# Moving the product of the gate's second half from sixth to fourth place in a seven-product feed-forward pair

## The chip, the cores and the metric

The kernel runs on one core of one Trainium2 chip. The metric is device time in microseconds for one execution, median of several. A profile of one execution gives, for each engine, when every instruction started and how long it took. The engines are called PE (TensorE's matmuls), PEld (its weight loads), DVE (VectorE), ACT (ScalarE), POOL (GpSimd) and SP (the queue that issues most DMAs).

## What is computed

The reference runs two transformer blocks of two layers each on one sequence of 512 tokens of width 1024. Layers differ in their mixers (mLSTM and neighbourhood attention, differential attention, HGRN2, forgetting attention, RG-LRU, stick-breaking attention), but each of the four layers ends in the same feed-forward part, and only that part is touched here:

```python
def swiglu(x, w_gu, w_down):
    gate, up = jnp.split(x @ w_gu, 2, axis=-1)
    return (jax.nn.silu(gate) * up) @ w_down
```

The hidden width is 2816, that is 22 blocks of 128. All of it is float32.

## The kernel before

Values lie transposed: 128 channels on the partitions, 512 tokens along the free side. A float32 factor is split into a high part (a copy by ACT into a reduced float32 type) and a low part (a subtraction by DVE), in the helper `split` at lines 271 to 278 (its copy is L273, its subtraction L275). A product of two split factors is three matmuls, high by high, high by low, low by high, issued by `mm3` (L283, L284, L285).

`ffn` (from L651) works through the 22 hidden blocks in three parts of 8, 7 and 7. A part first makes its hidden blocks, then multiplies them by its share of the down weights (L700 and on). The first three blocks of the first part are made in the plain way. The other 19 blocks of each layer, 76 in the kernel, are made by `seven` (L584 to L649), one call for each pair of a gate block and an up block. It is a scheme of Strassen's kind: gate and up for one hidden block are a 2 by 2 arrangement of half-size products (half the 1024 channels, half the 512 tokens), and seven such products replace eight. Each product is 12 matmuls of 128 x 128 weights by 256 columns (four channel blocks, three matmuls each).

In a call of `seven`, `g` and `u` are the gate and up weights as loaded by SP's queue (L607, L608). `a1` is the split of `g`. `ss` (from `s12`) and `a2` (from what is left in `u`) are splits of sums and differences of the halves of `g` and `u`, made by DVE on L612 to L617; `a4` is the split of the second half of `g` after L617. `b11`, `b12`, `b21`, `b22` are the four quarters of x, `t1` to `t4` are sums of them, made once in a feed-forward part (their high parts lie in the tile `ao`, their low parts in `t_l`). The products are, in the order in which the code writes them:

- P1: `a1` first half by `b11`, into the accumulator `pa` (a PSUM bank, tile `p_sc` in the profile). ACT copies `pa` to `keep[0]` (L630).
- P2: `ss` second half by `t2`, added onto `pa`. ACT copies `pa` to `keep[1]` (L633).
- P3: `ss` first half by `t1`, into `pz` (tile `p_tp`).
- P4: `a2` first half by `t3`, added onto `pa`. ACT copies `pa` to `keep[2]` (L636), and DVE adds `keep[2]` and `pz` into `c22` (L637).
- P5: `a1` second half by `b21`, into `pb` (tile `p_mm`). DVE adds `keep[0]` and `pb` (L639), ACT applies Silu (L640).
- P6: `a2` second half by `t4`, added onto `pa`. DVE multiplies it in (L642).
- P7: `a4` by `b22`, added onto `pz`, then L646 to L648 finish the second 256 tokens and `sink` splits the hidden block (tiles `f_h`, `f_l`).

`pa` thus holds a running sum that is read off three times in the middle of its accumulation: a product that adds onto `pa` can start only when the copy of the sum before it has ended. `seven` is a generator: `ffn` runs P1 of a pair, then P7 of the pair before, then P2 to P6, so TensorE sees P1, P7 of the pair before, P2, P3, P4, P5, P6, and then P1 of the next pair. The sets of weights are double-buffered: `a1` has two buffers, `ss` and `a2` share a ring of four.

What order an engine really issues in is decided by the layer under the kernel, which plans the whole program before it runs. For each engine it takes the instructions in the order of the program, but where the next one would have to wait by the planner's own estimate of durations, it puts a later one that is ready in its place, single matmuls too. That order is then fixed; on the chip each engine follows it and waits on semaphores.

Of the kernel before, what the change touches and what calls it, by code (L numbers as in the profile page):

```python
# [11 lines left out]
AF = mybir.ActivationFunctionType  # L12
ALU = mybir.AluOpType
# [193 lines left out]
class Prog:  # L207
# [376 lines left out]
    def seven(self, gate, up, pool, ts, sink):  # L584


        nc = self.nc
        t1, t2, t3, t4 = ts
        x = [[(self.XH[k][:, c], self.XL[k][:, c]) for k in range(4 * i, 4 * i + 4)] for i in range(2) for c in (slice(0, 256), slice(256, S))]
        b11, b12, b21, b22 = x  # L590
        h1, h2 = slice(0, 512), slice(512, 1024)

        def parts(src, own=None, bufs=4):

            tags, home, n = (("w_hi", "w_lo"), self.wp, 1024) if own is None else ((own + "h", own + "l"), pool, src.shape[1])
            hi, lo = (home.tile([P, n], F32R, name=i, tag=i, bufs=bufs) for i in tags)
            self.split(hi, lo, src)
            return hi, lo

        def product(ps, w, c, b, first, last):  # L600
            for k in range(4):
                ws = slice(c.start + k * P, c.start + (k + 1) * P)
                self.mm3(ps, (w[0][:, ws], w[1][:, ws]), b[k], first and k == 0, last and k == 3, skip_group_check=not (first and last))

        g = self.wp.tile([P, 1024], F32, name="w_raw", tag="w_raw", bufs=3)
        u = pool.tile([P, 1024], F32, name="u_raw", tag="u_raw", bufs=2)
        nc.sync.dma_start(out=g, in_=gate)  # L607
        nc.sync.dma_start(out=u, in_=up)  # L608
        a1 = parts(g, "a1", 2)
        s12 = pool.tile([P, 1024], F32, name="s12", tag="s12", bufs=1)  # L610

        nc.vector.tensor_tensor(s12[:, h1], u[:, h1], u[:, h2], ALU.add)  # L612
        nc.vector.tensor_tensor(s12[:, h2], s12[:, h1], g[:, h1], ALU.subtract)
        ss = parts(s12)
        nc.vector.tensor_tensor(u[:, h1], g[:, h1], u[:, h1], ALU.subtract)
        a2 = parts(u)
        nc.vector.tensor_tensor(g[:, h2], g[:, h2], s12[:, h2], ALU.subtract)  # L617

        pa = self.mm("sc")[:, 0:256]
        pz = self.mm("tp")[:, 0:256]  # L620
        pb = self.mm("mm")[:, 0:256]
        keep = []
        for name, bufs in (("k1", 1), ("k2", 2), ("k3", 1)):
            keep.append(pool.tile([P, 256], F32, name=name, tag=name, bufs=bufs))
        s = self.fp.tile([P, S], F32, name="f_s", tag="f_s", bufs=2)
        c22 = pool.tile([P, 256], F32, name="c22", tag="c22", bufs=1)
        c0, c1 = slice(0, 256), slice(256, S)

        product(pa, a1, h1, b11, True, False)
        nc.scalar.activation(keep[0], pa, AF.Copy)  # L630
        yield
        product(pa, ss, h2, t2, False, False)
        nc.scalar.activation(keep[1], pa, AF.Copy)  # L633
        product(pz, ss, h1, t1, True, False)
        product(pa, a2, h1, t3, False, False)
        nc.scalar.activation(keep[2], pa, AF.Copy)  # L636
        nc.vector.tensor_tensor(c22, keep[2], pz, ALU.add)  # L637
        product(pb, a1, h2, b21, True, True)
        nc.vector.tensor_tensor(s[:, c0], keep[0], pb, ALU.add)  # L639
        nc.scalar.activation(s[:, c0], s[:, c0], AF.Silu)  # L640
        product(pa, a2, h2, t4, False, True)
        nc.vector.tensor_tensor(s[:, c0], s[:, c0], pa, ALU.mult)  # L642
        a4 = parts(g[:, h2], "s4", 1)
        yield
        product(pz, a4, h1, b22, False, True)
        nc.vector.tensor_tensor(s[:, c1], keep[1], pz, ALU.add)  # L646
        nc.scalar.activation(s[:, c1], s[:, c1], AF.Silu)
        nc.vector.tensor_tensor(s[:, c1], s[:, c1], c22, ALU.mult)  # L648
        sink(s)  # L649
# [1072 lines left out]
```

## Time and profile before

| | us |
|---|---|
| Median of three runs | 2801.26 (2798.82 to 2802.35) |
| The profiled execution: its own time | 2803.35 |
| Its span, first to last instruction | 2801.6 |
| PE busy | 2751.7 (98%) |
| DVE busy | 2039.3 (73%) |
| ACT busy | 1513.2 (54%) |
| POOL busy | 415.8 (15%) |

The profiled execution's own time is 2.1 us above the median of the runs. Matmuls overlap in the records: one of 256 columns is recorded as 276 to 283 ns, while the next one starts 113 to 118 ns after it. The distance between starts, not the recorded length, is what a matmul costs.

### The profile page before, as it was taken

Reading aid. Unit: us, or ns where it says so; the run is one execution under the profiler, and the core shown is the slowest. Engines: PE = TensorE matmul, PEld = TensorE weight load, DVE = VectorE, ACT = ScalarE, POOL = GpSimd, SP = SyncE. Lnnn points to the kernel's source line nnn. Section 1 sums busy time; section 2 is a strip of 40 time slices with the busy share of each in tenths; the row PEclk is TensorE's granted clock in tenths of the full one; section 3 lists DMA queues with packets and bytes.
Section 4 is the critical chain, followed back from the end, with each engine's and each line's share of the span. In section 5 each row is a group of like instructions: output and inputs, shape, how many; then the busy total and the mean of one; then the engine's idle time right before and its main releaser. Section 6 shows DMA issues by size and latency. Waiting matters only on the chain. (4 is left out here: it accounts for less than half of the span.)

```text
span 2801.6 us, 46515 instructions
## 1 busy us (share of the span) xinstructions
PE 2751.7 (98%) x18090; PEld 2460.9 (88%) x18090; DVE 2039.3 (73%) x3560; ACT 1513.2 (54%) x2800; POOL 415.8 (15%) x500
## 2 busy tenths in 40 slices
PE   9999999999999999999999999999999999999998
PEld 7778989999987678899999988799999977898998
DVE  5877657776767888568667767778677758696785
ACT  4556545453556776455445544655445548663553
POOL 0412103000021122030000333240000301300003
PEclk9999999999999999999999999999999999999999
DMA  5232412323332225214232321224232321132322
GB/s 180 79 116 92 153 65 84 122 90 100 98 109 87 85 66 166 77 61 136 90 114 80 108 77 61 83 69 136 83 114 87 102 91 46 59 114 92 113 86 74
DMA packets 83103, 269.50 MB, mean 96 GB/s; under 512 B 10649, under 2 KB 15145, under 8 KB 82881
## 3 DMA queue, kind: packets, MB, share of 16 engines
q1 hardware_dynamic: 81376, 261.49, 28.8%
q0 software_dynamic: 1504, 5.04, 0.6%
q8 instruction: 142, 2.33, 0.3%
q14 instruction: 81, 0.66, 0.1%
HBM read 260.14 MB, written 2.15 MB: 94 GB/s over the span
## 5 line engine op out<-in xcount | busy, mean ns | idle before, releaser
L349 DVE TENSOR_TENSOR w_lo<-w_raw,w_hi 128x1024 fp32r<-128x1024 f32 (+3 forms) x440 | 412.2, 959 | 220.6 <-ACT w_hi L347 212.7
L347 ACT ACTIVATE w_hi<-w_raw 128x1024 fp32r<-128x1024 f32 (+2 forms) x326 | 331.6, 1024 | 364.5 <-PE p_mm L284 168.3
L283 PE MATMUL p_mm<-xh,w_hi 128*128 128x256 f32 (+1 forms) x1312 | 450.4, 344 | 9.6 <-ACT w_hi L347 5.1
L284 PE MATMUL p_mm<-xl,w_hi 128*128 128x256 f32 (+1 forms) x1312 | 447.5, 341 | 0.7 <-DVE xl L275 0.6
L285 PE MATMUL p_mm<-xh,w_lo 128*128 128x256 f32 (+1 forms) x1312 | 446.3, 340 | 0.0
L283 PEld LDWEIGHTS p_mm<-xh,w_hi 128*128 128x128 f32 x1312 | 248.9, 190 | 36.8 <-ACT w_hi L347 5.1
L284 PEld LDWEIGHTS p_mm<-xl,w_hi 128*128 128x128 f32 x1312 | 249.2, 190 | 29.0 <-DVE xl L275 1.7
L285 PEld LDWEIGHTS p_mm<-xh,w_lo 128*128 128x128 f32 x1312 | 249.2, 190 | 27.3 <-DVE w_lo L349 1.1
L510 POOL TENSOR_TENSOR ao<-xf 128x256 f32<-128x256 f32 x20 | 17.4, 871 | 1656.8 <-DVE xf L503 1227.8
L283 PE MATMUL p_sc<-ao,w_hi 128*128 128x256 f32 x912 | 256.5, 281 | 0.7 <-ACT k L630 0.7
L284 PE MATMUL p_sc<-t_l,w_hi 128*128 128x256 f32 x912 | 254.8, 279 | 0.0
L285 PE MATMUL p_sc<-ao,w_lo 128*128 128x256 f32 x912 | 254.8, 279 | 0.0
L283 PEld LDWEIGHTS p_sc<-ao,w_hi 128*128 128x128 f32 x912 | 173.1, 190 | 2.6 <-ACT k L630 2.5
L284 PEld LDWEIGHTS p_sc<-t_l,w_hi 128*128 128x128 f32 x912 | 171.4, 188 | 0.0
L285 PEld LDWEIGHTS p_sc<-ao,w_lo 128*128 128x128 f32 x912 | 171.2, 188 | 0.0
L284 PE MATMUL p_mm<-f_l,w_hi 128*128 128x512 f32 (+1 forms) x464 | 156.5, 337 | 1.4 <-DVE f_l L275 1.4
L283 PE MATMUL p_mm<-f_h,w_hi 128*128 128x512 f32 (+1 forms) x464 | 157.0, 338 | 0.0
L285 PE MATMUL p_sc<-f_h,w_lo 128*128 128x512 f32 (+1 forms) x464 | 156.4, 337 | 0.1
L283 PE MATMUL p_sc<-f_h,w_hi 128*128 128x512 f32 (+1 forms) x464 | 156.1, 337 | 0.0
L285 PE MATMUL p_mm<-f_h,w_lo 128*128 128x512 f32 (+1 forms) x464 | 156.1, 336 | 0.0
L284 PE MATMUL p_sc<-f_l,w_hi 128*128 128x512 f32 (+1 forms) x464 | 155.9, 336 | 0.0
L505 ACT ACTIVATE ao<-xf 128x256 f32<-128x256 f32 x160 | 64.8, 413 | 118.8 <-DVE xf L499 61.2
(497 smaller groups left out, 8011.5 us busy)
## 6 DMA issues: line engine op xcount, KB each, us to landing
w_raw<-in_f_gu SPq DMA_DIRECT2D x100, 512.0 KB, 3.6
u_raw<-in_f_gu SPq DMA_DIRECT2D x76, 512.0 KB, 3.5
w_raw<-in_w_e SPq DMA_DIRECT2D x70, 512.0 KB, 3.5
w_raw<-in_w_x SPq DMA_DIRECT2D x64, 512.0 KB, 3.9
w_raw<-in_w_o SPq DMA_DIRECT2D x64, 512.0 KB, 3.6
w_raw<-in_f_d SPq DMA_DIRECT2D x64, 448.0 KB, 3.3
w_raw<-in_f_d SPq DMA_DIRECT2D x32, 512.0 KB, 3.5
r_s<-r_t SPq DMA_DIRECT2D x64, 64.0 KB, 2.0
```

What stands on the lines that cost most here:

```text
L283: nc.tensor.matmul(out, wh, xh, start=start, stop=False, **kw)
L284: nc.tensor.matmul(out, wh, xl, start=False, stop=False, **kw)
L285: self.last = nc.tensor.matmul(out, wl, xh, start=False, stop=stop, **kw)
L347: nc.scalar.activation(hi[:, :n], raw[:, :n], AF.Copy)
L349: nc.vector.tensor_tensor(lo[:, c], raw[:, c], hi[:, c].bitcast(F32), ALU.subtract)
L505: square = nc.scalar.activation(x2, self.XF[m][:, c], AF.Square)
L510: eng.tensor_tensor(sm, self.XF[order[0]][:, c], self.XF[m][:, c], ALU.add)
```

## The change

P5, with the DVE addition and the Silu that follow from it, is moved from behind P4's read-out to in front of P3. No instruction is added or removed. The order that the code writes becomes P1, P7 of the pair before, P2, P5, P3, P4, P6: with P7 of the pair before counted in, the moved product comes fourth instead of sixth.

```diff
         yield
         product(pa, ss, h2, t2, False, False)
         nc.scalar.activation(keep[1], pa, AF.Copy)
+        product(pb, a1, h2, b21, True, True)
+        nc.vector.tensor_tensor(s[:, c0], keep[0], pb, ALU.add)
+        nc.scalar.activation(s[:, c0], s[:, c0], AF.Silu)
         product(pz, ss, h1, t1, True, False)
         product(pa, a2, h1, t3, False, False)
         nc.scalar.activation(keep[2], pa, AF.Copy)
         nc.vector.tensor_tensor(c22, keep[2], pz, ALU.add)
-        product(pb, a1, h2, b21, True, True)
-        nc.vector.tensor_tensor(s[:, c0], keep[0], pb, ALU.add)
-        nc.scalar.activation(s[:, c0], s[:, c0], AF.Silu)
         product(pa, a2, h2, t4, False, True)
```

## Rows read from the trace of the kernel before

**Rows 1.** The page's first part: busy time, share, instructions of each engine

```profile
PE 2751.7 (98%) x18090; PEld 2460.9 (88%) x18090; DVE 2039.3 (73%) x3560; ACT 1513.2 (54%) x2800; POOL 415.8 (15%) x500
```

**Rows 2.** Windows, six pairs in a row: length, each engine's busy time, granted clock

```profile
589.54:648.06 58.52, 58.52 (x506) 58.52 (x505) 49.39 (x80) 34.95 (x59) 0.00 (x0) 1.00 0.36 116
```

**Rows 3.** Timeline, PE, one pair's products (start, length, engine, line, tiles)

```profile
599.29 0.28 PE L283 MATMUL p_sc<-xh,a1h 128*128 128x256 f32 x1
...
600.66 0.28 PE L283 MATMUL p_tp<-xh,s4h 128*128 128x256 f32 x1
...
602.02 0.28 PE L283 MATMUL p_sc<-ao,w_hi 128*128 128x256 f32 x1
...
604.85 0.28 PE L283 MATMUL p_sc<-ao,w_hi 128*128 128x256 f32 x1
...
606.26 0.28 PE L283 MATMUL p_mm<-xh,a1h 128*128 128x256 f32 x1
...
607.68 0.28 PE L283 MATMUL p_sc<-ao,w_hi 128*128 128x256 f32 x1
...
609.05 0.28 PE L283 MATMUL p_sc<-xh,a1h 128*128 128x256 f32 x1
```

**Rows 4.** Timeline, PE, the first product of two neighbouring pairs, second layer

```profile
1293.21 0.28 PE L283 MATMUL p_sc<-xh,a1h 128*128 128x256 f32 x1
...
1302.91 0.28 PE L283 MATMUL p_sc<-xh,a1h 128*128 128x256 f32 x1
```

**Rows 5.** Timeline, ACT, beside the pair of Rows 3 (idle before, its releaser, in brackets)

```profile
604.42 0.63 ACT L273 ACTIVATE f_h<-f_s 128x512 fp32r<-128x512 f32 x1 [0.24 <-DVE f_s L648]
605.08 1.06 ACT L273 ACTIVATE w_hi<-s 128x1024 fp32r<-128x1024 f32 x1
606.52 0.38 ACT L636 ACTIVATE k<-p_sc 128x256 f32<-128x256 f32 x1 [0.38 <-PE p_sc L285]
607.76 1.06 ACT L273 ACTIVATE a1h<-w_raw 128x1024 fp32r<-128x1024 f32 x1 [0.85 <-PE p_mm L284]
608.73 0.40 ACT L640 ACTIVATE f_s<-f_s 128x256 f32<-128x256 f32 x1
```

**Rows 6.** Source line L636, the copy after P4: count, ns min/median/max

```profile
L636 ACT ACTIVATE k<-p_sc x76: 359/384/387, 494.3 to 2742.6; 128x256 f32<-128x256 f32 x76
```

**Rows 7.** Timeline, DVE, the low part of the next pair's `a1`

```profile
599.10 1.23 DVE L275 TENSOR_TENSOR a1l<-w_raw,a1h 128x1024 fp32r<-128x1024 f32 x1 [0.56 <-ACT a1h L273]
```

**Rows 8.** Timeline, first pair of a part: end of P1, copy, start of P2

```profile
582.13 0.28 PE L285 MATMUL p_sc<-xh,a1l 128*128 128x256 f32 x1
...
582.25 0.28 PE L283 MATMUL p_tp<-ao,w_hi 128*128 128x256 f32 x1
...
582.45 0.38 ACT L630 ACTIVATE k<-p_sc 128x256 f32<-128x256 f32 x1 [0.53 <-PE p_sc L285]
...
582.60 0.28 PE L283 MATMUL p_tp<-ao,w_hi 128*128 128x256 f32 x1
...
582.88 0.38 PE L283 MATMUL p_sc<-ao,w_hi 128*128 128x256 f32 x1
...
583.10 0.28 PE L284 MATMUL p_sc<-t_l,w_hi 128*128 128x256 f32 x1
```

**Rows 9.** Timeline, PE, another first pair: last matmul of P2, start of P4

```profile
491.81 0.28 PE L285 MATMUL p_sc<-ao,w_lo 128*128 128x256 f32 x1
...
492.61 0.38 PE L283 MATMUL p_sc<-ao,w_hi 128*128 128x256 f32 x1
492.83 0.28 PE L284 MATMUL p_sc<-t_l,w_hi 128*128 128x256 f32 x1
```

**Rows 10.** Timeline, first pair of the last layer: P1's end, copy, P2

```profile
2479.30 0.28 PE L285 MATMUL p_sc<-xh,a1l 128*128 128x256 f32 x1
...
2480.52 0.36 ACT L630 ACTIVATE k<-p_sc 128x256 f32<-128x256 f32 x1
...
2480.94 0.38 PE L283 MATMUL p_sc<-ao,w_hi 128*128 128x256 f32 x1 [0.66 <-ACT k L630]
```

## The prediction

> **What bounds the kernel now.** I read four views. The page's first part says that PE is busy 98% of the span [rows 1], so nothing that another engine gives up can shorten the run, unless PE waits for it. The windows over six pairs in a row say more for the stage at hand: PE and its weight loads are busy in all of 58.52 us, at the full granted clock, DVE in 49.39, ACT in 34.95 [rows 2]. The stage has no idle PE time that a new order could win back. The timeline of one pair shows the order on PE: P1 at 599.29, P7 of the pair before at 600.66, P2 at 602.02, P4 at 604.85, P5 at 606.26, P6 at 607.68, the next P1 at 609.05 [rows 3]. That is 9.76 us for 84 matmuls, 0.116 us from one start to the next. Last, the timeline of ACT beside it: the copy after P4 starts at 606.52 and takes 0.38 us [rows 5], so it ends at 606.90, while PE is in the middle of P5. P5 is what hides that copy: P6, which adds onto the bank being copied, starts only at 607.68, 0.78 us after the copy's end.
>
> **The change, part by part.** 76 pairs run through this code [rows 6]. The moved step is twelve matmuls, one DVE addition and one Silu; it issues no DMA, so nothing changes on SP's queue, and POOL does nothing in this stage [rows 2]. P5 reads `a1`, which P1 has used already, so it is as ready in its new place as in the old; its own twelve matmuls cost the same there. I put them at nothing, with the bounds of the next but one paragraph. The same holds for DVE's addition and the Silu: they come two products earlier, and PE doesn't wait for either.
>
> P4's own wait gets easier: between P2 and P4 there stand now P5 and P3, where P3 stood alone. That gains nothing in the steady pairs, where PE is busy throughout [rows 2]; in the first pair of a part of the first layer, P4 started late by 1.02 - 8 x 0.116 = 0.09 us from the matmul before it to its own second one [rows 9]. A few such pairs are under 1 us in all.
>
> What is lost is the cover over the copy after P4. In the new order P6 stands right behind P4 and must wait for that copy. Nothing of the kind stands in a steady pair of the trace, but the first pair of a part has it: there P2 follows P1 with no P7 between. P1's last matmul starts at 582.13, ACT's copy at 582.45 and takes 0.38, P2's first matmul starts at 582.88, 0.05 us after the copy, and its second one 0.22 us later, where 0.116 is usual [rows 8]. From the last matmul before the copy to the second one behind it this hand-over takes 0.97 us. In [rows 9] it is 492.83 - 491.81 = 1.02. For the copy after P4 itself I add up 1.03: P4's last matmul starts one spacing ahead of P5, at 606.14, its copy 0.38 after that [rows 3, 5], then 0.38 for the copy [rows 6], 0.05 and 0.22. I take 1.00.
>
> How much of that is lost depends on what the planner puts in the hole. PE follows the planned order, and behind P6 the next matmuls in program order are P1 of the next pair. They write another bank, and their weights are long there: the low part of `a1` for the P1 at 609.05 is done at 599.10 + 1.23 = 600.33 [rows 7]. So I expect the planner to put some of them between P4 and P6. How many is what [rows 8] shows for the same hole: four matmuls of a later product (the first at 582.25, the fourth at 582.60), and then P2, which the planner took to be ready. It believes the copy to be done sooner than it is. Four matmuls in the hole leave 1.00 - 6 x 0.116 = 0.30 us lost for each pair; by the ends 0.97 and 1.03, 0.27 to 0.33. With no matmul in the hole it would be 1.00 - 2 x 0.116 = 0.77, with six 0.07, with seven or more nothing. I take four, since the nearest row, the same copy with the same idle ACT, has four; none and seven stay as ends. In the last pair of a part there is no next P1, but the first matmuls of the down product, of 512 columns, are there; I count these pairs alike.
>
> 76 x 0.30 = 22.8 us (20.5 to 25 by the ends of the hand-over). The profiled execution took 2803.35 us, of which the span is 2801.6; with the change 2826.2, and since it lies 2.1 us above the median of the runs, 2824 for the median.
>
> The 0.22 us between the first two matmuls after the wait are part of that: the second one's weights are loaded only after the first has started [rows 8]. The Trainium skill, in "TensorE: Matmul & The Clock Gate", section "Step-by-step: what each phase is for", says that the engine's queue pulls weight loads ahead of matmuls in flight, so that the next weights load while the present matmul runs; by that the second matmul would come one spacing behind the first, 0.10 us less for each pair, and the sum would be some 8 us smaller, 2816. The trace shows the 0.22, so the sum above stands.
>
> Two costs that the trace shows only from the side. First, ACT ahead of the copy. In the new order P5's end frees the buffer of `a1`, so the 1.06 us split that now starts at 607.76, and the Silu of 0.40, come between P5 and the copy, together with the 1.06 us split of `w_hi` that P3's end releases [rows 5]. That is 2.52 us in the time of P3 and P4, 2 x 1.415 = 2.83 (P2 and P3 take 604.85 - 602.02) [rows 3]; the earlier split of `f_h` is over at 605.05, just behind what would be P5's end. Cover 0.3 us: I take no delay; if it is gone, the copy slips by what overruns, at most by one such split, 1.06 us. [rows 10] show such a case: with another split in front, the copy starts 1.22 us after the last matmul and P2 1.64 after it. Second, the pace of PE. Some products take 1.36 us, others 1.41 to 1.42 [rows 3], and in some parts a pair takes 9.70 instead of 9.76 [rows 4]. I have no cause for it. If the new order put all seven at 1.36, a pair would gain 9.76 - 9.52 = 0.24 us, 18 us in all; all at 1.42 would cost 0.18, 14 us. I take nothing for it.
>
> Who else waits when P6 waits: everything behind it on PE; L642 on DVE; the split of the `a2` two pairs on, whose buffer P6 frees. The latter two have a whole pair's time in hand, so only PE's queue counts. P7 now also follows L637, which follows the copy, but the rest of P1 and all of P6 lie between.
>
> **The rivals.**
>
> - *The hole is filled.* If the planner reckons ACT to be busy before the copy, it puts seven or more matmuls of P1 in the hole and nothing is lost: 2801, within 5 us; six would give 76 x 0.07 = 5 us more. For it: the first pair of the first layer had six matmuls between P2 and P4 and lost 0.09 us [rows 9]. Against it: [rows 8], where the planner stopped at four with ACT free. That the plan undoes the move (P5 put back behind P4, as filling) gives the same time; since P3 and P4 are ready in time, I see no reason for that.
> - *Faster.* PE's pace. P2, P3, P4 and P5 run at the slow pace in [rows 3], P6, P1 and P7 at the quick one. If the interruption before P6, or the new neighbours, leave all products at 1.36 us, the gain is 0.24 for each pair; it decides the sign as soon as the hole costs less than that, which is from five matmuls in it on (1.00 - 7 x 0.116 = 0.19). With the hole filled the time is 2783. For it: one pair in [rows 4] is 0.06 us shorter than that of [rows 3] with the same order. Against it: no pair runs all at 1.36.
> - *The full wait.* Nothing goes into the hole, or a wide split on ACT stands before the copy: 0.77 us for each pair, 58 us, 2860; with a copy that slips by 0.3 behind a filled hole of four, 0.6 us, 2847. For it: [rows 10]. Against it: the ready `a1` of [rows 7], and the cover reckoned above.
>
> **How the numbers follow.** The forecast of 2824 has a chance of 0.62; its own range, three to five matmuls in the hole (0.42 to 0.19 us for each pair), and the pace a little either way, is 2812 to 2836. The filled hole, with the plan that undoes the move, has 0.20, the faster case 0.06, the full wait 0.12. For all of it 8 times in 10 I go from 2799 to 2848: down through the filled hole, up to the slipped copy, and leave out the faster case and the full wait. About 0.2%, some 5.6 us, is what a measurement of this kernel can tell from no change. Faster by more than that 0.06, within it 0.20, slower 0.74.
>
> **What would show it.** In the timeline of PE after the change I expect P1, P7, P2, P5, P3, P4, four matmuls of the next P1, then P6 and the rest of P1; a weight load of P6 idle until L636; 0.22 us between P6's first two matmuls; 9.76 + 0.30 = 10.06 us from one P1 to the next. In the windows over six pairs PEld should show 0.2 us idle for each pair, ended by ACT's L636, and the source line L630 no more such waits than before. Seven or more matmuls of P1 in front of P6, or a pair of 9.8 us or less, would make the forecast wrong; so would a copy that starts much later than 0.38 us after P4's last matmul.

## The result: 0.7% slower, by the hole before P6

The changed kernel takes 2822.34 us (median of four runs, 2820.1 to 2824.74), the kernel before, run beside it on the same chip, 2801.81 (2798.82 to 2804.27). The ratio is 1.0072, with a 95% interval of 1.0059 to 1.0084: 20.5 us lost. The profiled execution took 2821.16 us, with a span of 2819.4, which is 17.8 us over that of before.

The page's first part, as [rows 1]:

```profile
PE 2760.7 (98%) x18090; PEld 2455.2 (87%) x18090; DVE 2037.7 (72%) x3560; ACT 1517.1 (54%) x2800; POOL 416.2 (15%) x500
```

The windows over six pairs in a row, as [rows 2] (length, busy time of PE, PEld, DVE, ACT, POOL, granted clock, DMA share, GB/s):

```profile
587.40:647.47 60.07, 59.67 (x507) 58.48 (x506) 48.35 (x79) 35.26 (x58) 0.00 (x0) 1.00 0.34 109
```

The window is 0.05 us longer than its six pairs: from the first pair's P1 at 587.38 to the down product that follows the sixth at 647.40 are 60.02 us, where before took 58.52, at the same full granted clock (1.00). That is 0.25 more for each. PE has 0.40 us without work in the window and PEld 1.59, where before both were busy throughout. The page's share of PE says 98% in both kernels: recorded lengths of matmuls overlap, so a hole in the stream of starts is nearly covered by the records on both sides. The timeline of PE over one pair shows the hole itself:

```profile
597.33 0.28 PE L283 MATMUL p_sc<-xh,a1h 128*128 128x256 f32 x1
...
600.42 0.28 PE L283 MATMUL p_tp<-xh,s4h 128*128 128x256 f32 x1
...
601.78 0.28 PE L283 MATMUL p_sc<-ao,w_hi 128*128 128x256 f32 x1
...
603.20 0.28 PE L283 MATMUL p_mm<-xh,a1h 128*128 128x256 f32 x1
...
604.61 0.28 PE L283 MATMUL p_tp<-ao,w_hi 128*128 128x256 f32 x1
...
605.98 0.28 PE L283 MATMUL p_sc<-ao,w_hi 128*128 128x256 f32 x1
...
607.23 0.28 PE L285 MATMUL p_sc<-ao,w_lo 128*128 128x256 f32 x1
607.34 0.28 PE L283 MATMUL p_sc<-xh,a1h 128*128 128x256 f32 x1
607.46 0.28 PE L284 MATMUL p_sc<-xl,a1h 128*128 128x256 f32 x1
607.57 0.28 PE L285 MATMUL p_sc<-xh,a1l 128*128 128x256 f32 x1
607.68 0.28 PE L283 MATMUL p_sc<-xh,a1h 128*128 128x256 f32 x1
608.04 0.38 PE L283 MATMUL p_sc<-ao,w_hi 128*128 128x256 f32 x1
608.26 0.29 PE L284 MATMUL p_sc<-t_l,w_hi 128*128 128x256 f32 x1
```

The order is P7 of the pair before at 600.42, P2 at 601.78, P5 at 603.20, P3 at 604.61, P4 at 605.98, then four matmuls of the next P1 (607.34 to 607.68), P6 at 608.04. From 597.33 to 607.34, the same place in the next pair, are 10.01 us, where [rows 3] have 9.76. Between the fourth matmul of P1 and P6 lie 0.36 us, between P6's first and second 0.22. The timeline of ACT beside it, as [rows 5]:

```profile
604.69 1.06 ACT L273 ACTIVATE a1h<-w_raw 128x1024 fp32r<-128x1024 f32 x1 [0.24 <-PE p_mm L284]
605.66 0.40 ACT L636 ACTIVATE f_s<-f_s 128x256 f32<-128x256 f32 x1
606.07 1.06 ACT L273 ACTIVATE w_hi<-s 128x1024 fp32r<-128x1024 f32 x1
607.60 0.38 ACT L639 ACTIVATE k<-p_sc 128x256 f32<-128x256 f32 x1 [0.47 <-PE p_sc L285]
```

And the source line of the copy after P4 (L639 now), as [rows 6], with who waited for it (us, times):

```profile
L639 ACT ACTIVATE k<-p_sc x76: 383/383/386, 493.8 to 2761.0; 128x256 f32<-128x256 f32 x76
...
  PEld p_sc L283: 20.1, 76
```

ACT has been idle for 0.47 us when P4 ends, copies from 607.60 to 607.98, and P6 starts 0.06 later. P6's first weight load waits for this copy in all 76 pairs, 20.1 us together, 0.26 each.

### The profile page after: what moved, and what is told of

It is laid out like the page before. It is cut to its first block, busy times and chain, and to the rows that moved or that the text cites. A ratio compares the mean times of both kernels' runs of the same rounds, so it can differ in the third digit from the quotient of the medians.

```text
span 2819.4 us, 46419 instructions
## 1 busy us (share of the span) xinstructions
PE 2760.7 (98%) x18090; PEld 2455.2 (87%) x18090; DVE 2037.7 (72%) x3560; ACT 1517.1 (54%) x2800; POOL 416.2 (15%) x500
## 5 line engine op out<-in xcount | busy, mean ns | idle before, releaser
L283 PE MATMUL p_sc<-ao,w_hi 128*128 128x256 f32 x912 | 262.7, 288 | 5.0 <-ACT k L630 0.4
L283 PEld LDWEIGHTS p_sc<-ao,w_hi 128*128 128x128 f32 x912 | 172.1, 189 | 22.5 <-ACT k L639 20.1
L273 ACT ACTIVATE w_hi<-u_raw 128x1024 fp32r<-128x1024 f32 x76 | 80.6, 1061 | 139.3 <-PE p_sc L284 134.7
```

Source lines behind the costliest of these rows:

```text
L273: x = nc.scalar.activation(hi, src, AF.Copy, scale=scale)
L283: nc.tensor.matmul(out, wh, xh, start=start, stop=False, **kw)
```

## The experiments

The theory was the prediction's: the whole loss is the hand-over from P4 over ACT's copy to P6, 1.0 us, less what PE has to do in it. Its rivals were a cost of the earlier P5 itself, and a cost that follows the copy whatever stands beside it. Each ratio is to the kernel before, run beside the experiment: 2802.12 us (median) for the first four, 2799.95 for the last two, which ran on another chip. Steady pairs are here those behind the first one of a part, or behind the first two of a layer's first part: 48 in the kernel, each measured from its P1 to the next.

**P3 behind P4.** P5 keeps its new place; only P3 is moved back, as a cover between P4 and P6.

```diff
-        product(pz, ss, h1, t1, True, False)
         product(pa, a2, h1, t3, False, False)
         nc.scalar.activation(keep[2], pa, AF.Copy)
+        product(pz, ss, h1, t1, True, False)
         nc.vector.tensor_tensor(c22, keep[2], pz, ALU.add)
```

> The changed kernel with P3 moved behind P4's copy, so that P5 stays in fourth place (P1, P7 of the pair before, P2, P5, P4, P3, P6) but twelve matmuls of P3 stand in the hole before P6. Theory (the loss is the uncovered hand-over from P4 over ACT's copy to P6): the hole is covered again, about 2801 as before the change, a pair 9.75 us. Rival (the early place of P5 itself costs, by what it brings to ACT and DVE sooner): stays at about 2822. On PE's pace: in both traces the spacing of matmuls flips between 0.113 and 0.118 us where PE passes from a product with x to one with the t sums. If that is the rule, the flips here are at P2 and P4, and either P2 and P5 alone run slowly (two products where the kernel before has four: 2 x 0.055 x 76 = 8 us less, 2793) or the other five do (4 us more, 2806).

Measured: 2805.73 us (2803.23 to 2809.57), ratio to before 1.0013 (1.0004 to 1.0022). The timeline of PE has P4, P3, P6 and the next P1:

```profile
605.18 0.28 PE L283 MATMUL p_sc<-ao,w_hi 128*128 128x256 f32 x1
...
606.55 0.28 PE L283 MATMUL p_tp<-ao,w_hi 128*128 128x256 f32 x1
...
607.91 0.28 PE L283 MATMUL p_sc<-ao,w_hi 128*128 128x256 f32 x1
608.03 0.28 PE L284 MATMUL p_sc<-t_l,w_hi 128*128 128x256 f32 x1
...
609.27 0.28 PE L283 MATMUL p_sc<-xh,a1h 128*128 128x256 f32 x1
```

P6 follows P3 without a hole, its second matmul 0.12 behind its first, and no wait for the copy after P4 is left. 40 steady pairs take 9.65 us, eight 9.81. So the early P5 costs nothing in the steady pairs; 17 of the 20.5 us go with the cover. Where P2 and P5 alone run slowly, as in the 40, the expectation had 2793 us, and that didn't come: the median is 3.6 us over before. In the trace the eight later parts take 6.0 us less than in before (from P1 of the first pair to P7 of the last), the four first parts 3.8 more. One place where that goes is the second pair of a layer's first part. The timeline there, of ACT and of PE's weight loads:

```profile
497.52 1.06 ACT L273 ACTIVATE w_hi<-s 128x1024 fp32r<-128x1024 f32 x1 [2.91 <-DVE s L613]
498.51 1.07 ACT L273 ACTIVATE w_hi<-u_raw 128x1024 fp32r<-128x1024 f32 x1
499.48 0.36 ACT L630 ACTIVATE k<-p_sc 128x256 f32<-128x256 f32 x1
...
499.89 0.19 PEld L283 LDWEIGHTS p_sc<-ao,w_hi 128*128 128x128 f32 x1 [0.46 <-ACT k L630]
```

Two wide splits stand ahead of the copy after P1, so that copy ends after P7 does, and P2's load waits 0.46 us. The 3.6 us themselves can't be placed in this trace: the profiled execution is the fastest of its eleven, and its span of 2801.5 us is that of before. The late copy is the slip that the prediction feared for the copy after P4, at another copy.

**An empty hole.** The order of after, but the planner may not put the next pair's P1, P5 or P3 ahead of P6. The diff shows P1; P5 and P3 are wrapped in the same way.

```diff
+        turn = ExitStack()
+        if behind is not None:
+            turn.enter_context(self.tc.issue_after(behind.ins))
+        with turn:
-        product(pa, a1, h1, b11, True, False)
+            product(pa, a1, h1, b11, True, False)
...
         product(pa, a2, h2, t4, False, True)
+        self.p6 = self.last
```

> The changed kernel, but the next pair's P1, P5 and P3 may be issued only behind P6, so that nothing stands in the hole (the last pair of each part, 12 of 76, may still take matmuls of the down product). Theory: the hand-over of 1.03 us is seen less two spacings, 1.03 - 2 x 0.116 = 0.80 us for each of 64 pairs, 0.3 for the other 12: 55 us above the kernel before, 2856, a pair 10.5 us. Rival (four matmuls ahead of P6 do not help, the loss of 0.27 has another cause): stays at 2822.

Measured: 2849.56 us (2849.3 to 2849.99), ratio 1.0168 (1.0154 to 1.0182). The timeline has P4's last matmul, the copy, and P6:

```profile
608.16 0.28 PE L285 MATMUL p_sc<-ao,w_lo 128*128 128x256 f32 x1
608.54 0.38 ACT L652 ACTIVATE k<-p_sc 128x256 f32<-128x256 f32 x1 [0.47 <-PE p_sc L285]
...
608.97 0.39 PE L283 MATMUL p_sc<-ao,w_hi 128*128 128x256 f32 x1 [0.53 <-ACT k L652]
...
609.20 0.28 PE L284 MATMUL p_sc<-t_l,w_hi 128*128 128x256 f32 x1
```

From 608.16 to 609.20 are 1.04 us, of which two spacings of 0.115 are work: 0.81 lost. Steady pairs take 10.47, 0.46 more than in after, which is what four matmuls are worth (4 x 0.115). So the four matmuls in the hole are what keeps the loss of after small. The sum over the kernel is 64 x (10.47 - 9.75) = 46 us; the last pair of each of the 12 parts still has the down product to fill with. 47.4 were measured. The expectation had 55: it left out that PE's pace gives some 0.09 us back in each pair, and took 0.3 for the last pairs, which is too much (both below).

**Six matmuls of P5 in the hole.** P5 is cut in two: its first six matmuls stay ahead of P3, the other six stand between P4 and P6, with the addition and the Silu behind them.

```diff
-        product(pb, a1, h2, b21, True, True)
-        nc.vector.tensor_tensor(s[:, c0], keep[0], pb, ALU.add)
-        nc.scalar.activation(s[:, c0], s[:, c0], AF.Silu)
+        product(pb, a1, h2, b21, True, False, range(0, 2))
...
         nc.vector.tensor_tensor(c22, keep[2], pz, ALU.add)
+        product(pb, a1, h2, b21, False, True, range(2, 4))
+        nc.vector.tensor_tensor(s[:, c0], keep[0], pb, ALU.add)
+        nc.scalar.activation(s[:, c0], s[:, c0], AF.Silu)
```

> The changed kernel with P5 cut in two: its first two channel blocks, six matmuls, in fourth place, the other six between P4's copy and P6, with the addition and the Silu behind them. Theory: six matmuls in the hole leave 1.03 - 8 x 0.116 = 0.10 us for each pair, 8 us above the kernel before, 2809; the planner adds nothing to the six. Rival (a hole costs the same whatever its filling): 2822; rival (any filling covers it): 2801. PE's pace may shift it by 5 us either way, since a third passage from x to the t sums is added.

Measured: 2806.03 us (2803.68 to 2808.75), ratio 1.0014 (1.0005 to 1.0023). The timeline of PE has P4's last matmul, the first and the last of the six, and P6's first two:

```profile
606.73 0.28 PE L285 MATMUL p_sc<-ao,w_lo 128*128 128x256 f32 x1
...
606.85 0.28 PE L283 MATMUL p_mm<-xh,a1h 128*128 128x256 f32 x1
...
607.41 0.28 PE L285 MATMUL p_mm<-xh,a1l 128*128 128x256 f32 x1
...
607.54 0.39 PE L283 MATMUL p_sc<-ao,w_hi 128*128 128x256 f32 x1
...
607.76 0.28 PE L284 MATMUL p_sc<-t_l,w_hi 128*128 128x256 f32 x1
```

The hand-over is again 1.03 us (606.73 to 607.76). Eight spacings of it are work, 0.11 is lost, and nearly all of that is the 0.22 between P6's first two matmuls. With none, four, six and twelve matmuls in the hole, the loss per pair by the rows is thus 0.81, 0.34, 0.11 and nothing: 1.03 less the work, as the prediction reckoned it. For the step from six to twelve the rows alone speak: 2806.03 us is no longer than the 2805.73 with P3 as a full cover, and the steady pair takes 9.76, as in before, since the better pace gives back what the hole takes.

**P6 into a bank of its own.** Nothing waits for a read-out any more; DVE adds the two sums.

```diff
-        product(pa, a2, h2, t4, False, True)
-        nc.vector.tensor_tensor(s[:, c0], s[:, c0], pa, ALU.mult)
+        product(pd, a2, h2, t4, True, True)
+        nc.vector.tensor_tensor(k4, keep[2], pd, ALU.add)
+        nc.vector.tensor_tensor(s[:, c0], s[:, c0], k4, ALU.mult)
```

> The changed kernel, but P6 goes into a PSUM bank of its own and DVE adds it to keep[2] in one more instruction (0.41 us for each pair, 31 us of DVE time in all) before the multiplication. P6 no longer adds onto the bank that ACT copies, so it has nothing to wait for. Theory: no hand-over, 2801, or 2793 if only P2 and P5 run at the slow pace; DVE's extra work hides, since it is busy 49 of 58.5 us in this stage. Rival (P5's early place or a crowded ACT costs): 2822. Rival (DVE becomes the bound): above 2822.

Measured: 2807.69 us (2803.44 to 2811.83), ratio 1.0017 (1.0008 to 1.0026). The wait is gone, so most of the loss is; but the time lies above both values expected. The timeline of PE has P4's last matmul and P6's first:

```profile
607.67 0.28 PE L285 MATMUL p_sc<-ao,w_lo 128*128 128x256 f32 x1
607.79 0.28 PE L283 MATMUL p_sc<-ao,w_hi 128*128 128x256 f32 x1
```

P6 follows P4 in the usual spacing, and all 48 steady pairs take 9.81 us: P2 and P5 take 1.36 us each, the other five products 1.41 to 1.42 (2 x 1.36 + 5 x 1.415 = 9.80). The expectation counted on the pace of the kernels before, and the pace is another one here; the last experiment is about that. It accounts for 48 x 0.06 = 3 of the 6 us. Most of the others lie in the four first parts, which take 2.7 us more than in before.

**The copy twice.** ACT reads P4's bank out two times, first into a buffer that nobody reads.

```diff
         product(pa, a2, h1, t3, False, False)
+        nc.scalar.activation(k4, pa, AF.Copy)
         nc.scalar.activation(keep[2], pa, AF.Copy)
```

> The kernel after, but ACT reads P4's bank out twice behind P4: first into a further buffer that nothing reads, then, as before, into the one that DVE adds from. P6 must wait for both. The copy is thus doubled: by the 0.29 us by which a second copy would start behind the first with ACT already at work, up to the 0.38 us that one takes. The planner knows of the second copy, and its planned order has seven matmuls of the next P1 in the hole where the kernel after has four. Theory (the loss is the gap between the copy's real hand-over and what the planner takes it to be, not the copy's length): hand-over 1.03 + 0.29 to 0.38 = 1.32 to 1.41 us, of which nine spacings of 0.116 are work, so 0.28 to 0.37 us lost for each pair against the kernel before, about that of the kernel after: 2821 to 2829 us, a ratio to before of 1.007 to 1.010. Rival (each pair pays for the length of the copy between P4 and P6, whatever stands in the hole): 0.30 + 0.29 to 0.38 us for each pair, 45 to 52 us over before: 2847 to 2854 us, 1.016 to 1.019.

Measured: 2822.61 us (2821.98 to 2823.21), ratio 1.0078 (1.0063 to 1.0093): within the interval the same as after, with twice the copies. The timeline from P4's last matmul on, PE and ACT's two copies:

```profile
610.20 0.28 PE L285 MATMUL p_sc<-ao,w_lo 128*128 128x256 f32 x1
...
610.32 0.28 PE L283 MATMUL p_sc<-xh,a1h 128*128 128x256 f32 x1
...
610.58 0.38 ACT L640 ACTIVATE k<-p_sc 128x256 f32<-128x256 f32 x1 [0.47 <-PE p_sc L285]
...
610.86 0.38 ACT L641 ACTIVATE k<-p_sc 128x256 f32<-128x256 f32 x1
...
611.00 0.28 PE L283 MATMUL p_sc<-xh,a1h 128*128 128x256 f32 x1
...
611.29 0.38 PE L283 MATMUL p_sc<-ao,w_hi 128*128 128x256 f32 x1
...
611.51 0.28 PE L284 MATMUL p_sc<-t_l,w_hi 128*128 128x256 f32 x1
```

The hand-over grew to 1.31 us (610.20 to 611.51), by the 0.28 between the two copies' starts. But the planner knew of the second copy and put seven matmuls of P1 in the hole instead of four, so nine spacings of 0.114 are work and 0.28 is lost. The rival, by which each pair pays for the length of the copy (2847 to 2854 us), falls: what a pair loses is the part of the hand-over that the planner left unfilled.

**One passage between x and t.** On PE's two paces, which the sums above run into. A passage is here a place where PE goes over from a product that moves x (tiles `xh`, `xl`) to one that moves a sum `t` (tiles `ao`, `t_l`). P6 has its own bank, as two experiments before this one, and P5 stands ahead of P2; the diff is against that kernel.

```diff
         yield
-        product(pa, ss, h2, t2, False, False)
-        nc.scalar.activation(keep[1], pa, AF.Copy)
         product(pb, a1, h2, b21, True, True)
         nc.vector.tensor_tensor(s[:, c0], keep[0], pb, ALU.add)
         nc.scalar.activation(s[:, c0], s[:, c0], AF.Silu)
+        product(pa, ss, h2, t2, False, False)
+        nc.scalar.activation(keep[1], pa, AF.Copy)
```

> On the two paces of PE's 128x256 matmuls, 113 and 118 ns from start to start. P6 has a bank of its own (so nothing waits for a copy), and P5 stands ahead of P2: the order is P1, P7 of the pair before, P5, then P2, P3, P4, P6. PE so passes only once in a pair from products that move xh and xl (P1, P7, P5) to those that move the transposed parts (P2, P3, P4, P6). In the kernels so far it passes twice in a pair, and the pace was seen to change at both passages, so that each pair is alike. Theory (the pace changes at every such passage): the pace now changes once in a pair, so pairs alternate, one near 84 x 0.1133 = 9.52 us and the next near 84 x 0.118 = 9.91, mean 9.72, which is 7 us less over 76 pairs than with P6 in its own bank and P5 behind P2 (2807.7): about 2801, ratio to before 0.999 to 1.000. Rival (the pace belongs to the kind of product or to its place beside the others): all pairs of a part alike, with the same products slow in each; 9.65 to 9.81, 2796 to 2808.

Measured: 2802.78 us (2798.75 to 2805.76), ratio 1.0009 (0.9999 to 1.0018). The timeline of PE, the first matmul of P2 in four pairs in a row:

```profile
592.92 0.28 PE L283 MATMUL p_sc<-ao,w_hi 128*128 128x256 f32 x1
...
602.45 0.28 PE L283 MATMUL p_sc<-ao,w_hi 128*128 128x256 f32 x1
...
612.35 0.28 PE L283 MATMUL p_sc<-ao,w_hi 128*128 128x256 f32 x1
...
621.88 0.28 PE L283 MATMUL p_sc<-ao,w_hi 128*128 128x256 f32 x1
```

The distances are 9.53, 9.90 and 9.53 us, and so they go on, in turn, through the second and third parts of all four layers; the first parts hold one or two longer pairs (10.16 to 10.34) each, around which the turn isn't regular. Pairs of one and the same order, with the same products, differ by 0.37 us, so the pace belongs neither to a product nor to its neighbours: it changes once at each passage. That rests on these rows; the time lies in the rival's range too (2796 to 2808). None of the orders tried is faster than the kernel before beyond its interval.

## Why the prediction was right

The forecast of 2824 with a chance of 0.62 was made from the mechanism that the trace shows: P6 waits for the copy behind P4, and four matmuls stand in the hole. Its terms can be taken one by one.

- *The order.* P1, P7, P2, P5, P3, P4, four matmuls of the next P1, P6: as written. The four came from [rows 8], a hole of the same kind in the first pair of a part; it was read off there and not worked out. That the planner reckons the copy shorter than it is fits a second case: with the copy doubled it added three matmuls, and 0.28 was lost still. The planner's own estimates stand in no run.
- *The hand-over.* 1.00 was taken, between ends of 0.97 and 1.03. The steady pair has 608.26 - 607.23 = 1.03, the value summed up for this copy itself; the rows of a neighbouring copy were the worse guide. Less six spacings of 0.115 it is 0.34 lost, not 0.30.
- *The 0.22 us between P6's first two matmuls* was kept in the sum. The rows of after have it (608.04 to 608.26), those of the empty hole and of the doubled copy too (608.97 to 609.20, 611.29 to 611.51). P6's first two weight loads in after:

```profile
608.04 0.19 PEld L283 LDWEIGHTS p_sc<-ao,w_hi 128*128 128x128 f32 x1 [0.28 <-ACT k L639]
608.15 0.19 PEld L284 LDWEIGHTS p_sc<-t_l,w_hi 128*128 128x128 f32 x1
```

  The second load starts 0.11 us after the first matmul; in P4, without a wait, a load starts together with the matmul ahead of its own (both at 607.12). The Trainium skill ("TensorE: Matmul & The Clock Gate", section "Step-by-step: what each phase is for") has weight loads pulled ahead of matmuls in flight, when the row groups don't conflict or the load goes to the background weight buffer. By that rule the time would have been 2816, by the prediction's estimate; the lowest run is 2820.1, and behind this wait the trace doesn't show it. Whether the page's conditions held here, no run tells.
- *Pace, taken at nothing.* This term was mis-sized. A pair of 10.01 us less the hand-over of 1.03 is 8.98 us for 78 spacings, 0.1151 each, where before had 0.1162: 84 x 0.0011 = 0.09 us gained for each pair. P2 and P5 alone run at the slow pace now, where P2 to P5 did before. 0.34 - 0.09 is the 0.25 by which the pair got longer.
- *The last pairs, counted alike.* Not quite. There three matmuls of the down product fill the hole, and they are twice as wide. The timeline of PE:

```profile
647.28 0.28 PE L285 MATMUL p_sc<-ao,w_lo 128*128 128x256 f32 x1
647.40 0.39 PE L283 MATMUL p_mm<-f_h,w_hi 128*128 128x512 f32 x1
647.63 0.40 PE L284 MATMUL p_mm<-f_l,w_hi 128*128 128x512 f32 x1
647.86 0.40 PE L285 MATMUL p_mm<-f_h,w_lo 128*128 128x512 f32 x1
648.10 0.39 PE L283 MATMUL p_sc<-ao,w_hi 128*128 128x256 f32 x1
648.32 0.28 PE L284 MATMUL p_sc<-t_l,w_hi 128*128 128x256 f32 x1
```

  Of 1.04 us, 3 x 0.233 + 2 x 0.115 = 0.93 are work; 0.11 is lost in each of these 12. By the rows the loss is 64 x 0.25 + 12 x (0.11 - 0.09) = 16 us, by the spans 17.8, by the medians 20.5; the prediction had 22.8. Spans and medians differ by where the two profiled executions lie, that of before 1.5 us above its median, that of after 1.2 below. The prediction's errors on the small side (the hand-over) and on the large side (pace, last pairs) cancelled in part, so the pair was right to 0.05 us. That the total came within 2.3 us of the medians is in part luck: the rows bear out only 16.
- *What would show it.* 10.06 us from one P1 to the next was expected, 10.01 came; PEld idle 0.2 us for each pair, 1.59 / 6 = 0.27 came; nine weight loads wait for the copy of L630, as many as before; the 0.22 us and the order stand above.
- *ACT ahead of the copy.* Cover of 0.3 us was reckoned, 0.47 is there: the Silu starts while the split before it is still in its record (604.69 + 1.06 lies past 605.66), so lengths in a row sum to more than ACT takes. The copy didn't slip.
- *The rivals.* The filled hole needed seven matmuls and got four; the empty hole, forced, gave 2849.6, where the prediction's full wait was 2860, since the 12 last pairs are filled even so and the pace is better. The faster case named the pace rightly as able to move with the order, but it moved by 0.09, not 0.24.

## What to carry to other kernels

Where one accumulator is read out in the middle, count the matmuls that stand between the last one before the read-out and the first one behind it: here it would take seven of 256 columns to hide the 1.03 us (nine spacings of 0.115, an estimate that no run tried), and a whole independent product of twelve did. A planner that fills holes by its own estimates makes such a step cheaper, not free: what is left is what it leaves unfilled of the hand-over, and the place to look for it is a weight load that waits in every pair, since PE's busy share reads 98% with the hole and without. An order is to be understood by the distance between starts over a whole period, product by product, for the pace alone can move a pair by 0.1 us, as much as a hole with six matmuls costs. It is to be judged by the kernel's time: with P3 behind P4 most steady pairs were 0.10 us shorter than before, and the kernel was 3.6 us longer.

## What the runs showed of the hardware

Matmuls of 256 columns run at two paces, 0.113 and 0.118 us from start to start, at the same full granted clock (1.00 in the windows of before and after). In the steady pairs of every kernel looked at, the pace changes where PE passes, without waiting, from a product that moves `xh` and `xl` (P1, P5, P7) to one that moves `ao` and `t_l` (P2, P3, P4, P6), and not at the passage back. So before has a slow section P2 to P5 and a quick one P6, P1, P7; after has P2, P5 slow and the rest quick; with P6 in its own bank the same two are quick and the rest slow; and with one passage in a pair whole pairs alternate, 9.53 and 9.90. Where PE waits at a passage, the rule doesn't hold: in after's steady pairs the pace stays at 0.113 from P1's four matmuls to P6, and in the first pair of a layer's later parts, where P5's first four stand ahead of P2, it goes from 0.118 before the wait (581.52) to 0.113 behind it (582.15). Which section is the slow one depends on how the stretch began, and can differ between parts of one kernel: the 9.70 of [rows 4] against 9.76 is this: there P2 to P5 are quick and P6, P1, P7 slow. Only the rule is shown; why a passage changes the pace is open. The weights change their tiles at the same passages (from `a1` and `s4` to `w_hi` and `w_lo`), so it may be the weights as well as what moves, and no run here changed the tiles' places or the banks by themselves. For a reader of such a trace it means that a new order can gain or lose some 0.1 us in a pair of 9.7 with no wait anywhere.
